# First mixer's convolution: 64x64 products in the four corners of the TensorE array, in place of 128x128 products

## The chip, the cores and the metric

The kernel runs on one core of one Trainium2 chip. The metric is the device time of one execution in microseconds (us). The profile is of one execution of the same program, taken by the hardware profiler. Engines are named as in the profile: PE is TensorE (products), PEld its loading of stationary operands, DVE is VectorE, ACT is ScalarE, POOL is GpSimd, and SP is the engine from whose queue nearly all DMAs are issued.

## The reference, cut to what matters

Two residual layers over 1024 positions of width 1024, float32. The first layer's mixer has two parallel parts, a convolution module and an mLSTM memory with four heads, behind one input projection and one output projection. What the change touches is the convolution module: 512 channels, each with a causal filter of 31 taps along the sequence, then a bias, a layer norm over the 512 channels and SiLU.

```python
z = h @ w_in
ca, cg, q, k, v, og, gates = jnp.split(z, cuts, -1)
u = ca * jax.nn.sigmoid(cg)
u = causal_depthwise_conv(u, conv_w, conv_b)      # 31 taps, one filter for each channel
u = jax.nn.silu(layernorm(u, ln_g, ln_b))
...
return jnp.concatenate([u, hm], -1) @ w_out
```

## The kernel before, in words

**The whole.** `trunk_kernel` runs `mixer0` (convolution and mLSTM), a feed-forward block, `mixer1` (gated linear attention), and a second feed-forward block. Almost all products are the projections: each operand is split into a high and a low part, and `mm3` (lines 174 to 176) adds three products for each pair, so that L174, L175 and L176 are the three products of one step of a projection. Weights come in with a DMA from SP (L164), ACT rounds them to the high part `wH` (L167) and DVE makes the low part `wL` (L168). The tags `wH` and `wL` have three buffers each.

**The order of the work.** `ORDER0` lists the steps of `mixer0`. Those that matter here are `c0` to `c3` (`conv_in`: the projection to 128 channels of `u`, and its store to DRAM), `v0` to `v3` (`conv`: the filter itself on these 128 channels), `g` (values and output gates of a head, `head_vo`, L548 and L549 read its banks), `x` (a head's recurrence, L623 to L645) and `l` (`layer_norm`). In `ORDER0` stand `v0 x0a v1 x0b g1` and later `v2 x1a v3 x1b l g2`. A scheduler in the language's layer turns program order and priorities (`high_priority`, offset `WOFF`) into one fixed list of instructions for each engine when the program is built. On the chip every engine works through its list in order and waits on semaphores.

**The filter as products.** Position t is 8n + s, with phase s from 0 to 7 and n from 0 to 127. `conv_in` stores `u` to DRAM as channel, phase, n (`ud`). `conv(i)` handles 128 channels in two halves `j` of 64. It loads a half as tile `ur`: 16 channels times 8 phases fill the 128 partitions, and four such groups lie side by side (L403; two buffers, `GB`). Taps reach back 30 positions, so at most four steps of n: for each group, five products (m from 0 to 4, L411) of a stationary 128x128 block with a 128-column window of `ur` shifted by m add up in PSUM. The stationary block maps (channel, phase in) to (phase out, channel). It is zero wherever the channels differ, so 15 of 16 of its elements are zero. The blocks of one group are a tile `cw` of 128x640 (L408), which takes a buffer of the tags `wH` and `wL` in turn. In all there are 4 (i) x 2 (j) x 4 (e) x 5 (m) = 160 products in float32 of 128x128 by 128 columns. Both operands are plain float32 here, and the trace shows each such product as two loads and two passes, so 320 rows. The four groups of a half fill one PSUM bank (`sm`, four buffers), which DVE reads with the bias (L413) into `y`.

**Behind it.** `layer_norm` sums over the channels by adding `y` tiles and by a product with `ones_p`, a matrix that says which partitions hold the same phase (built from `e4`, L359 to L365). The result goes to DRAM (`zd`, L449, 32 DMAs) and comes back channel-major (L455).

Of the kernel before, what the change touches and what calls it, by code (L numbers as in the profile page):

```python
# [8 lines left out]
F32 = mybir.dt.float32  # L9
# [7 lines left out]
P = 128  # L17
# [5 lines left out]
TAPS = 31  # L23
PH = 8
CG = 16
NT = T // PH
SH = 4
# [11 lines left out]
WOFF = 200  # L39
# [11 lines left out]
GB = 2  # L51
# [28 lines left out]
def trunk_kernel(ctx, tc, xT, cols, gate_b0, ev_vo0, ev_u, ev_cw, ev_out, od_v0, od_u, od_out, gate_w2, fin_row,  # L80
# [13 lines left out]
    def nm(s):  # L94
        uid[0] += 1
        return f"{s}_{uid[0]}"

    def bank(tag):
        return ps.tile([P, 512], F32, tag=tag, name=nm(tag))
# [7 lines left out]
    b = bank("sm")  # L107
# [186 lines left out]
    def mixer0(cut, then):  # L294
        with tc.tile_pool(name="m0", bufs=1, reuse_waits="tile") as mp:
# [62 lines left out]

            e4 = mp.tile([PH, PH, CG], F32, tag="e4", name="e4")  # L359
            DVE.tensor_copy(e4, ident[:PH, :PH].unsqueeze(2).to_broadcast([PH, PH, CG]))  # L360
            b = bank("sm")[:, :P]
            e4 = e4.rearrange("e a c -> e (a c)")
            PE.matmul(b, e4, e4, start=True, stop=True)
# [29 lines left out]
            def conv(i):  # L393


                for j in range(2):
                    b = bank("sm")
                    y = xy(2 * i + j if i < 2 else 2 * i + j - 4, int(i > 1))
                    Y.append(y)
                    with tc.high_priority(offset=WOFF):  # L400
                        raw = mp.tile([P, 4, NT + SH], F32, tag="ur", name=nm("ur"), bufs=GB)
                        DVE.memset(raw[:, :, :SH], 0.0)
                        SP.dma_start(raw[:, :, SH:], ud[i][j * 64:(j + 1) * 64].rearrange("(g c) s n -> (c s) g n", g=4))  # L403
                    for e in range(4):
                        g = 8 * i + 4 * j + e
                        with tc.high_priority(offset=WOFF):
                            w = wp.tile([P, 1088], F32, tag="wL" if e % 2 else "wH", name=nm("cw"))[:, :(SH + 1) * P]
                            SP.dma_start(w, ev_cw[g])  # L408
                        o = b[:, e * NT:(e + 1) * NT]
                        for m in range(SH + 1):  # L410
                            PE.matmul(o, w[:, m * P:(m + 1) * P], raw[:, e, m:m + NT], start=m == 0, stop=m == SH)  # L411
                    g = 8 * i + 4 * j
                    DVE.tensor_tensor(out=by_phase(y), in0=by_phase(b),  # L413
                                      in1=col[:, C_CB + g:C_CB + g + 4].unsqueeze(2).to_broadcast([P, 4, NT]), op=ALU.add)
# [11 lines left out]
            def layer_norm():  # L426
# [19 lines left out]
                for j, y in enumerate(Y):  # L446
                    DVE.tensor_tensor(out=by_phase(y), in0=by_phase(y), in1=r.unsqueeze(1).to_broadcast([P, 4, NT]), op=ALU.mult)
                    for e in range(4):
                        SP.dma_start(zd[4 * j + e].rearrange("c a n -> a c n"), y[:, e * NT:(e + 1) * NT])  # L449

# [1408 lines left out]
def _layout(i):  # L1859
# [17 lines left out]
    def phased(v):  # L1877

        return np.tile(v.reshape(-1, CG).T, (PH, 1))


    cw = i["ev_conv_w"][0].reshape(TAPS, 32, CG)
    band = np.zeros((32, CG, PH, SH + 1, PH, CG), np.float32)
    for c in range(CG):
        for m in range(SH + 1):
            for sp in range(PH):
                for ap in range(PH):
                    j = PH * (m - SH) + sp - ap + TAPS - 1
                    if 0 <= j < TAPS:
                        band[:, c, sp, m, ap, c] = cw[j, :, c]  # L1890
    band = band.reshape(32, P, (SH + 1) * P)
    qw = i["ev_qk_conv_w"][0].reshape(4, 8, P).transpose(2, 1, 0).reshape(P, 32)
# [4 lines left out]
    e = i["ev_w_in"][0]  # L1897
# [91 lines left out]
```

## Time and profile before

| | |
|---|---|
| median of 3 runs | 2112.51 us (2112.13 to 2113.88) |
| the profiled execution, device time | 2112.64 us |
| the profiled execution, span from first to last instruction | 2110.9 us |
| granted TensorE clock over the span | 0.998 |
| the filter's products (L411) on PE, in four pieces | 150.4 to 171.6 us and 221.3 to 242.4 us |
| passes of the filter on PE | 320 |
| DMAs of the filter's weights (`cw`) | 32 of 320 KB |
| DMAs of the filter's input (`ur`) | 8 of 256 KB |

A row of the groups reads: line, engine, operation, tile written and tiles read (buffer numbers left out), shapes, count, then busy time in us and the mean of one in ns, then the idle time of the engine just ahead. Products are pipelined, so the duration of one pass (some 275 ns) is longer than the distance from one pass to the next. That distance is what counts, and it is taken from the timeline, where rows of one line that follow each other are merged: start, length of the whole piece, and count. The length runs from the first start to the last end.

### The profile page before, as it was taken

Reading aid. Unit: us, or ns where it says so; the run is one execution under the profiler, and the core shown is the slowest. Engines: PE = TensorE matmul, PEld = TensorE weight load, DVE = VectorE, ACT = ScalarE, POOL = GpSimd, SP = SyncE. Lnnn points to the kernel's source line nnn. Section 1 sums busy time; section 2 is a strip of 40 time slices with the busy share of each in tenths; the row PEclk is TensorE's granted clock in tenths of the full one; section 3 lists DMA queues with packets and bytes.
Section 4 is the critical chain, followed back from the end, with each engine's and each line's share of the span. In section 5 each row is a group of like instructions: output and inputs, shape, how many; then the busy total and the mean of one; then the engine's idle time right before and its main releaser. Section 6 shows DMA issues by size and latency. Waiting matters only on the chain.

```text
span 2110.9 us, 27850 instructions
## 1 busy us (share of the span) xinstructions
PE 2094.3 (99%) x10367; PEld 1773.9 (84%) x10367; DVE 1508.4 (71%) x2296; ACT 866.7 (41%) x1411; POOL 2.9 (0%) x15
## 2 busy tenths in 40 slices
PE   9999999999999999999999999999999999999998
PEld 8889989888888888888889978888888888888887
DVE  7555788677776666867875577666877666677686
ACT  6212327443222232444546545644522232234553
POOL 0000000000000000000000000000000000000000
PEclk9999999999999999999999999999999999999999
DMA  4324454545443233834546643454544333374344
GB/s 157 96 98 136 148 129 121 200 167 178 169 156 109 90 105 131 293 97 133 165 133 218 201 146 119 170 179 149 190 155 166 114 105 110 101 273 145 96 129 146
DMA packets 154636, 312.57 MB, mean 148 GB/s; under 512 B 24128, under 2 KB 37312, under 8 KB 154496
## 3 DMA queue, kind: packets, MB, share of 16 engines
q1 hardware_dynamic: 154224, 310.48, 44.5%
q8 instruction: 83, 1.36, 0.3%
q14 instruction: 57, 0.47, 0.1%
q10 hardware_dynamic: 272, 0.26, 0.0%
HBM read 229.91 MB, written 80.77 MB: 147 GB/s over the span
## 4 chain that ended last, share of the span: by engine, by line
PE 96%; ACT 1%; DVE 1%; DMA 1%; issue 0%; SPq 0%; DVEq 0%; ACTq 0%
PE mm L174 20%; PE mm L175 20%; PE mm L176 20%; PE sm L176 10%; PE sm L174 10%; PE sm L175 10%; PE sm L411 2%; PE sm L1266 1%; PE sm L1268 1%; PE sm L1265 0%; DVE bs L1053 0%; PE sm L624 0%; PE sm L1293 0%; PE sm L1254 0%; PE sm L591 0%; PE sm L626 0%
## 5 line engine op out<-in xcount | busy, mean ns | idle before, releaser
L175 PE MATMUL mm<-hL,wH 128*128 128x512 f32 x1356 | 531.3, 392 | 0.3 <-DVE hL L339 0.3
L176 PE MATMUL mm<-hH,wH 128*128 128x512 f32 x1356 | 529.5, 391 | 0.0
L174 PE MATMUL mm<-hH,wL 128*128 128x512 f32 x1356 | 492.9, 392 | 3.4 <-ACT hH L338 1.5
L174 PEld LDWEIGHTS mm<-hH,wL 128*128 128x128 f32 x1356 | 254.5, 188 | 58.4 <-ACT hH L338 2.3
L175 PEld LDWEIGHTS mm<-hL,wH 128*128 128x128 f32 x1356 | 255.1, 188 | 53.2 <-DVE hL L339 0.6
L176 PEld LDWEIGHTS mm<-hH,wH 128*128 128x128 f32 x1356 | 254.9, 188 | 53.2 <-issue 0.2
L175 PE MATMUL sm<-hL,wH 128*128 128x512 f32 x616 | 240.1, 390 | 0.0
L176 PE MATMUL sm<-hH,wH 128*128 128x512 f32 x616 | 239.7, 389 | 0.0
L174 PE MATMUL sm<-hH,wL 128*128 128x512 f32 x616 | 209.0, 390 | 0.0
L147 ACT ACTIVATE wH<-S 128x1024 fp32r<-128x1024 f32 x97 | 102.8, 1060 | 232.9 <-PE sm L176 213.6
L147 ACT ACTIVATE wH<-q 128x512 fp32r<-128x512 f32 x143 | 90.3, 632 | 179.2 <-PE mm L176 98.8
L147 DVE TENSOR_TENSOR wL<-q,wH 128x512 fp32r<-128x512 f32 x143 | 98.6, 690 | 70.6 <-ACT wH L147 70.3
L147 ACT ACTIVATE wH<-raw 128x1024 fp32r<-128x1024 f32 (+1 forms) x90 | 89.9, 1000 | 122.2 <-PE sm L176 68.1
L147 DVE TENSOR_TENSOR wL<-S,wH 128x1024 fp32r<-128x1024 f32 x97 | 118.5, 1221 | 26.3 <-ACT wH L147 26.3
L175 PEld LDWEIGHTS sm<-hL,wH 128*128 128x128 f32 x616 | 115.6, 188 | 24.7 <-issue 0.7
L174 PEld LDWEIGHTS sm<-hH,wL 128*128 128x128 f32 x616 | 115.6, 188 | 24.5 <-PE mm L176 0.5
L176 PEld LDWEIGHTS sm<-hH,wH 128*128 128x128 f32 x616 | 115.6, 188 | 24.3 <-issue 0.2
L175 PE MATMUL mm<-wL,hH 128*128 128x256 f32 (+2 forms) x480 | 136.0, 284 | 0.0
L176 PE MATMUL mm<-wH,hH 128*128 128x256 f32 (+2 forms) x480 | 135.9, 285 | 0.0
L174 PE MATMUL mm<-wH,hL 128*128 128x256 f32 (+2 forms) x480 | 135.8, 286 | 0.1
L1493 DVE TENSOR_TENSOR c<-sm,c 128x512 f32<-128x512 f32 x110 | 75.6, 687 | 72.0 <-PE sm L176 72.0
L147 DVE TENSOR_TENSOR wL<-raw,wH 128x1024 fp32r<-128x1024 f32 (+1 forms) x90 | 103.5, 1150 | 13.2 <-ACT wH L147 13.2
(355 smaller groups left out, 3577.2 us busy)
## 6 DMA issues: line engine op xcount, KB each, us to landing
raw<-in_w SPq DMA_DIRECT2D x108, 512.0 KB
mdT<-c SPq DMA_DIRECT2D x88, 256.0 KB
m<-mdT SPq DMA_DIRECT2D x88, 256.0 KB
mdB<-c SPq DMA_DIRECT2D x66, 256.0 KB
raw<-in_od_u SPq DMA_DIRECT2D x32, 512.0 KB
q<-in_w SPq DMA_DIRECT2D x60, 256.0 KB
m<-mdB SPq DMA_DIRECT2D x55, 256.0 KB
raw<-in_ev_u SPq DMA_DIRECT2D x20, 512.0 KB
```

The lines of the kernel that those rows point to most:

```text
L147: ins = ACT.activation(dst[0], src, AF.Copy), lo.tensor_tensor(out=dst[1], in0=src, in1=dst[0], op=ALU.subtract)
L174: return (PE.matmul(o, lt[1], rt[0], start=start and not on, stop=False, skip_group_check=on), PE.matmul(o, lt[0], rt[1], start=False, sto ...
L175: PE.matmul(o, lt[0], rt[1], start=False, stop=False, skip_group_check=on),
L176: PE.matmul(o, lt[0], rt[0], start=False, stop=stop, skip_group_check=on))
L411: PE.matmul(o, w[:, m * P:(m + 1) * P], raw[:, e, m:m + NT], start=m == 0, stop=m == SH)
L1266: PE.matmul(ob[:, cc, :], A[:, cs], v[:, c, :], start=True, stop=st is None)
L1268: PE.matmul(ob[:, cc, :], q[:, cs], st, start=False, stop=True)
L1493: DVE.tensor_tensor(out=out, in0=a, in1=b, op=ALU.add)
```

## The change

Each product now has 64 rows and 64 columns of the array. Eight channels times eight phases fill 64 partitions; the block is still zero where channels differ (7 of 8 elements). The two halves `j` of `conv(i)` are no longer worked one after the other. They lie on partitions 0 to 63 and 64 to 127 of one tile `ur` with one buffer (128 x 8 groups x 132), loaded by two DMAs of 64 partitions. For each of four weight tiles (`e`) and each m, four products follow: two groups of eight channels (`hc`), which write partitions 0 to 63 or 64 to 127 of a bank, times two halves (`j`), which write one bank each. So the four products of a step use the four corners of the array. In all there are 4 x 4 x 5 x 2 x 2 = 320 products of 64x64 by 128 columns, in place of 160 of 128x128. There are 16 DMAs of weights of 128x640 in place of 32. The two banks of a `conv(i)` are finished together. Partitions of `y` are now (channel, phase) in place of (phase, channel), and `e4`, the bias columns and the store to `zd` follow that.

```diff
-            e4 = mp.tile([PH, PH, CG], F32, tag="e4", name="e4")
-            DVE.tensor_copy(e4, ident[:PH, :PH].unsqueeze(2).to_broadcast([PH, PH, CG]))
+            e4 = mp.tile([PH, CG, PH], F32, tag="e4", name="e4")
+            DVE.tensor_copy(e4, ident[:PH, :PH].unsqueeze(1).to_broadcast([PH, CG, PH]))
...
             def conv(i):
-                for j in range(2):
-                    b = bank("sm")
+                with tc.high_priority(offset=WOFF):
+                    raw = mp.tile([P, 8, NT + SH], F32, tag="ur", name=nm("ur"), bufs=1)
+                    DVE.memset(raw[:, :, :SH], 0.0)
+                    for j in range(2):
+                        SP.dma_start(raw[64 * j:64 * j + 64, :, SH:],
+                                     ud[i][64 * j:64 * j + 64].rearrange("(g c) s n -> (c s) g n", g=8))
+                bs = [bank("sm") for _ in range(2)]
+                for e in range(4):
+                    with tc.high_priority(offset=WOFF):
+                        w = wp.tile([P, 1088], F32, tag="wL" if e % 2 else "wH", name=nm("cw"))[:, :(SH + 1) * P]
+                        SP.dma_start(w, ev_cw[4 * i + e])
+                    for m in range(SH + 1):
+                        for hc in range(2):
+                            for j, b in enumerate(bs):
+                                rows = slice(64 * j, 64 * j + 64)
+                                o = (hc * (SH + 1) + m) * 64
+                                PE.matmul(b[64 * hc:64 * hc + 64, e * NT:(e + 1) * NT], w[rows, o:o + 64],
+                                          raw[rows, 2 * e + hc, m:m + NT], start=m == 0, stop=m == SH)
+                for j, b in enumerate(bs):
                     y = xy(2 * i + j if i < 2 else 2 * i + j - 4, int(i > 1))
                     Y.append(y)
-                    with tc.high_priority(offset=WOFF):
-                        raw = mp.tile([P, 4, NT + SH], F32, tag="ur", name=nm("ur"), bufs=GB)
-                        DVE.memset(raw[:, :, :SH], 0.0)
-                        SP.dma_start(raw[:, :, SH:], ud[i][j * 64:(j + 1) * 64].rearrange("(g c) s n -> (c s) g n", g=4))
-                    for e in range(4):
-                        g = 8 * i + 4 * j + e
-                        with tc.high_priority(offset=WOFF):
-                            w = wp.tile([P, 1088], F32, tag="wL" if e % 2 else "wH", name=nm("cw"))[:, :(SH + 1) * P]
-                            SP.dma_start(w, ev_cw[g])
-                        o = b[:, e * NT:(e + 1) * NT]
-                        for m in range(SH + 1):
-                            PE.matmul(o, w[:, m * P:(m + 1) * P], raw[:, e, m:m + NT], start=m == 0, stop=m == SH)
...
-                        SP.dma_start(zd[4 * j + e].rearrange("c a n -> a c n"), y[:, e * NT:(e + 1) * NT])
+                        SP.dma_start(zd[4 * j + e].rearrange("c a n -> (c a) n"), y[:, e * NT:(e + 1) * NT])
...
-    cw = i["ev_conv_w"][0].reshape(TAPS, 32, CG)
-    band = np.zeros((32, CG, PH, SH + 1, PH, CG), np.float32)
-    for c in range(CG):
+    cw = i["ev_conv_w"][0].reshape(TAPS, 4, 2, 4, 2, CG // 2).transpose(0, 1, 3, 2, 4, 5)
+    band = np.zeros((4, 4, 2, CG // 2, PH, 2, SH + 1, CG // 2, PH), np.float32)
+    for c in range(CG // 2):
...
-                        band[:, c, sp, m, ap, c] = cw[j, :, c]
-    band = band.reshape(32, P, (SH + 1) * P)
+                        band[:, :, :, c, sp, :, m, c, ap] = cw[j, ..., c]
+    band = band.reshape(16, P, 2 * (SH + 1) * 64)
```

The scheduler also gives PE another order around the filter. Behind the change, line numbers from 417 on are higher by four. The first place is PE's list from the end of `conv(0)` to the start of `conv(1)`; `ur_1443` is `conv(1)`'s input before. Before:

```order
L411 MATMUL sm_1364<-ur_1366,cw_1390 128x128 x5
L623 MATMUL sm_1398<-v_436,kw_1328 128x129
L624 MATMUL sm_1399<-v_436,rb_1307 128x129 x2
L623 MATMUL sm_1419<-v_436,kw_1328 128x129
L624 MATMUL sm_1420<-v_436,rb_1307 128x129
L623 MATMUL sm_1398<-v_436,kw_1328 128x129
L626 MATMUL sm_1399<-st_1402,qk_1067 128x129
L626 MATMUL sm_1420<-st_1407,qk_1067 128x129
L624 MATMUL sm_1420<-v_436,rb_1307 128x129
L411 MATMUL sm_1441<-ur_1443,cw_1446 128x128 x5
```

After, the last products of `conv(0)` and what follows them; `wH_1634` and `wL_1635` are the first weights of `head_vo(1)`:

```order
L411 MATMUL sm_1335<-ur_1330,cw_1402 64x128
L627 MATMUL sm_1428<-v_436,kw_1328 128x129
L628 MATMUL sm_1429<-v_436,rb_1307 128x129 x2
L174 MATMUL mm_1650<-wH_1634,hL_26_156 128x256
L174 MATMUL mm_1677<-wH_1634,hL_26_156 128x256
L174 MATMUL mm_1704<-wH_1634,hL_26_156 128x256
L174 MATMUL mm_1731<-wH_1634,hL_26_156 128x256
L627 MATMUL sm_1449<-v_436,kw_1328 128x129
L175 MATMUL mm_1650<-wL_1635,hH_25_155 128x256
L176 MATMUL mm_1650<-wH_1634,hH_25_155 128x256
```

So 48 of the 192 products of `head_vo(1)` now stand between the two pieces of the filter (42 of them behind the last row shown), beside the nine products of the recurrence that stood there before. The same holds for `head_vo(2)` between `conv(2)` and `conv(3)`.

The second place is DVE's list behind `conv(0)`; `sm_1334` and `sm_1335` are its two banks. Before, the reads of the banks (L413) and the clearing of the next inputs' margins (L402), with `conv(1)`'s banks `sm_1441` and `sm_1475`, and the low weights of `head_vo(1)`:

```order
L413 TENSOR_TENSOR xy_220_1442<-sm_1441,col 128x512
L402 MEMSET ur_1989 128x4x4
L168 TENSOR_TENSOR wL_1575<-raw_1572,wH_1574 128x1024
L431 TENSOR_TENSOR s_2229<-s_2229,xy_220_1442 128x512
L168 TENSOR_TENSOR wL_1581<-raw_1578,wH_1580 128x1024
L413 TENSOR_TENSOR xy_227_1476<-sm_1475,col 128x512
```

After, right behind `conv(0)`:

```order
L417 TENSOR_TENSOR xy_198_1424<-sm_1334,col 128x512
L397 MEMSET ur_1471 128x8x4
L168 TENSOR_TENSOR wL_1635<-raw_1632,wH_1634 128x1024
L417 TENSOR_TENSOR xy_199_1426<-sm_1335,col 128x512
L633 COPY st_1432<-sm_1428 128x129
```

The low part `wL` of the first weights of `head_vo(1)` has moved from the middle of `conv(1)` to the end of `conv(0)`, between the reads of `conv(0)`'s two banks. Its buffer is that of the last weights of `conv(0)` (`cw_1402`), so it cannot be written before `conv(0)` is through.

The third place is SP's list of DMAs, from the last weights of `conv(0)` on. Before, weights and input halves alternate:

```order
L408 DMA cw_1446<-in_ev_cw 128x640
L403 DMA ur_1443<-ud 128x4x128
L408 DMA cw_1453<-in_ev_cw 128x640
L408 DMA cw_1460<-in_ev_cw 128x640
L408 DMA cw_1467<-in_ev_cw 128x640
L408 DMA cw_1480<-in_ev_cw 128x640
L403 DMA ur_1477<-ud 128x4x128
```

After, all weights of `conv(1)` come first, and both halves of its input (`ur_1471`) together, when `conv(0)` has read the only buffer for the last time:

```order
L405 DMA cw_1499<-in_ev_cw 128x640
L405 DMA cw_1477<-in_ev_cw 128x640
L405 DMA cw_1521<-in_ev_cw 128x640
L391 DMA ud<-u_1195 128x1024
L405 DMA cw_1543<-in_ev_cw 128x640
L399 DMA ur_1471<-ud 64x8x128 x2
L164 DMA raw_1868<-in_ev_u 128x1024
```

Behind the tail of `mixer0` the lists of all engines are the same as before but for a few neighbouring products of one projection that change places.

More of the change, by code (lines that the diff above doesn't have):

```diff
@@ L357, in mixer0 @@
                                pattern=[[1, P]], channel_multiplier=-1)
-            e4 = mp.tile([PH, PH, CG], F32, tag="e4", name="e4")
-            DVE.tensor_copy(e4, ident[:PH, :PH].unsqueeze(2).to_broadcast([PH, PH, CG]))
+            e4 = mp.tile([PH, CG, PH], F32, tag="e4", name="e4")
+            DVE.tensor_copy(e4, ident[:PH, :PH].unsqueeze(1).to_broadcast([PH, CG, PH]))
             b = bank("sm")[:, :P]
-            e4 = e4.rearrange("e a c -> e (a c)")
+            e4 = e4.rearrange("e c a -> e (c a)")
             PE.matmul(b, e4, e4, start=True, stop=True)
@@ L1877, in phased @@
     def phased(v):
-        return np.tile(v.reshape(-1, CG).T, (PH, 1))
-    cw = i["ev_conv_w"][0].reshape(TAPS, 32, CG)
-    band = np.zeros((32, CG, PH, SH + 1, PH, CG), np.float32)
-    for c in range(CG):
+        return np.repeat(v.reshape(-1, CG).T, PH, axis=0)
+    cw = i["ev_conv_w"][0].reshape(TAPS, 4, 2, 4, 2, CG // 2).transpose(0, 1, 3, 2, 4, 5)
+    band = np.zeros((4, 4, 2, CG // 2, PH, 2, SH + 1, CG // 2, PH), np.float32)
+    for c in range(CG // 2):
         for m in range(SH + 1):
```

## The prediction

> **What bounds the kernel.** First the page's busy times and the shares of the chain of work that ended last:
>
> ```profile
> PE 2094.3 (99%) x10367; PEld 1773.9 (84%) x10367; DVE 1508.4 (71%) x2296; ACT 866.7 (41%) x1411; POOL 2.9 (0%) x15
> PE 96%; ACT 1%; DVE 1%; DMA 1%; issue 0%; SPq 0%; DVEq 0%; ACTq 0%
> ```
>
> PE is the chain: of 2110.9 us of span it lacks only 16.6 us. Next the stretch in which the filter runs, 150 to 260 us, in the table by stage (busy PE, PEld, DVE, ACT, POOL, then granted clock, DMA share, GB/s), and the shares of the chain from 140 to 260 us:
>
> ```profile
> 150.00:260.00 110.00, 109.56 (x854) 105.12 (x853) 65.47 (x143) 27.58 (x77) 0.00 (x0) 1.00 0.49 156
> by line: PE sm L411 29.8%; PE mm L176 18.9%; PE mm L175 18.9%; PE mm L174 18.8%; PE sm L624 3.3%; PE sm L591 3.0%; PE sm L626 2.7%; PE sm L623 2.6%; PE sm L596 1.3%; DVE st L632 0.6%; PE sm L424 0.2%; issue 0.1%
> ```
>
> PE stands still for 0.44 us there, at full clock, and L411, the filter, holds 29.8% of 120 us, 35.8 us. DVE is busy for 60% and so has room. So a nanosecond of PE time won or lost in the filter is one of the whole, until something else is late.
>
> **The filter's passes.** The timeline of PE gives the distance from pass to pass, and the groups of instructions (shapes kept apart) the duration of one:
>
> ```profile
> 150.43 9.10 PE L411 MATMUL sm<-ur,cw 128*128 128x128 f32 x80
> 150.00 0.60 PE L596 MATMUL sm<-ident,qk 128*128 128x128 f32 x4
> 78.78 0.78 PE L518 MATMUL sm<-ident,row 4*128 4x4 f32 x10
> 78.78 0.69 PEld L518 LDWEIGHTS sm<-ident,row 4*128 4x128 f32 x10 [0.35 <-issue]
> ```
> ```profile
> L411 PE MATMUL sm<-ur,cw 128*128 128x128 f32 x320 | 36.7, 275 | 0.0
> L1266 PE MATMUL sm<-v,A 128*128 128x256 f32 x64 | 18.5, 379 | 0.0
> L411 PEld LDWEIGHTS sm<-ur,cw 128*128 128x128 f32 x320 | 36.2, 192 | 0.0
> L596 PEld LDWEIGHTS sm<-ident,qk 128*128 128x128 f32 x28 | 3.3, 141 | 0.0
> L489 PEld LDWEIGHTS sm<-ident,gz 128*36 128x36 f32 x8 | 0.7, 98 | 0.2
> L1063 PEld LDWEIGHTS sm<-ident,least 128*1 128x1 f32 x1 | 0.1, 84 | 0.0
> L518 PEld LDWEIGHTS sm<-ident,row 4*128 4x128 f32 x24 | 1.9, 136 | 2.0 <-issue 1.4 <-DVE wL L168 0.4 <-DVE row L512 0.2
> ```
>
> Of the first row, the last pass alone takes 0.275 us, so 79 distances fill 9.10 - 0.275 us: 111.7 ns each (112 below), and 320 of them make 35.7 us. Two things ask for these 112 ns. A pass of 256 columns takes 104 ns more than one of 128 (379 against 275), so 128 columns stream for some 104 ns. The load of 128 float32 columns takes 192 ns where that of one column takes 84, so 108 ns are the columns, 0.85 ns each. Load and stream lie beside each other, or the distance would be twice as long. Both are full.
>
> The change makes 640 passes and 640 loads of 64 columns. A stream is as long as before (128 columns). A load has 84 + 64 x 0.85 = 138 ns, which is what L518's load has (136; a transpose loads a column in about half the time: 98 ns for 36 columns, 141 for 128). L518's products have four columns, so its row shows such loads with next to nothing beside them: (0.69 - 0.136) / 9 = 62 ns from load to load. All columns to be loaded together are as many as before (640 x 64 = 320 x 128). The change halves the streams, if four run at a time, but not the loads. Four cases follow for the filter's 35.7 us:
>
> (a) Loads go one after the other, as in every row of the trace: 640 x 62 ns = 39.7 us, 4.0 us more.
> (b) Loads of different corners overlap, but products start in order. A float32 product is two passes in one corner (320 rows for 160 products). The second waits for the first's 104 ns, and the next product's first pass can go beside it, no earlier. So one product per 111.7 ns: 320 x 111.7 ns = 35.7 us, nothing gained.
> (c) Every corner goes its own way: 80 rounds of two passes at 111.7 ns, 17.9 us, a gain of 17.9 us.
> (d) Nothing overlaps: 640 x 111.7 ns = 71.5 us, 35.7 us more.
>
> I take (a). It needs no behaviour that the trace does not show, L518 is the nearest row, and where (a) and (b) both hold the slower one counts. Its ends are (b)'s 35.7 us and 39.7 us.
>
> The Trainium skill (TensorE: Matmul & The Clock Gate, Part 3, on packing small matmuls) has products in different corners start about 4 ns apart and run side by side. That taken alone gives (c). The same section has products start and finish strictly in program order, which with two passes in one corner gives (b). Neither is shown by a run here, and the trace has no two products that share the array.
>
> **Changing the shape.** PE goes into the 64x64 products and out of them ten times (twice around each `conv`, once more because a first product of `conv(1)` stands alone). The trace has no such change; the nearest is from L518's loads of four rows to a full projection:
>
> ```profile
> 79.49 0.50 PE L175 MATMUL mm<-hL,wH 128*128 128x512 f32 x1
> ```
>
> L518's last pass starts 0.198 us (its duration) before its piece ends at 79.56, so at 79.36; the projection starts 0.13 us on, about its load's 108 ns. So I take nothing. The other end is that a pass must be through before the next load begins, 275 - 112 = 163 ns each, 1.6 us. The Trainium skill (TensorEngine Tiling (Array Packing), Tiling Modes, Key Properties) says that changing the tiling mode drains TensorE; by it the sum is those 1.6 us higher. No row here shows it.
>
> **The new order around the filter.** Behind `conv(0)` PE now runs a product L623 and two of L624 (six passes of 112 ns), four L174 of 256 columns, another L623, and then an L175 that needs `wL_1635`. DVE makes that between the reads of the two banks.
>
> ```profile
> 173.05 0.28 PE L174 MATMUL mm<-wH,hL 128*128 128x256 f32 x1
> 174.96 0.28 PE L175 MATMUL mm<-wL,hH 128*128 128x256 f32 x1
> 159.59 0.67 DVE L413 TENSOR_TENSOR xy<-sm,col 128x512 f32<-128x512 f32 x1 [3.79 <-issue]
> 160.18 0.28 DVE L629 COPY st<-sm 128x129 f32<-128x129 f32 x1
> L168 DVE TENSOR_TENSOR wL<-raw,wH x67: 1199/1225/1294, 24.1 to 1455.9; 128x1024 fp32r<-128x1024 f32 x63, 128x1056 fp32r<-128x1056 f32 x2, 128x1088 fp32r<-128x1088 f32 x2
> PE sm L626 <- DVE st L632: 0.4, 2, 0.2
> ```
>
> Sixteen projection passes take 1.91 us, 0.12 each. So PE reaches the L175 8 x 0.112 + 4 x 0.12 = 1.4 us after the filter's last start. DVE begins the bank read when that pass has ended (9.10 us after 150.43, at 159.53, the read at 159.59), some 0.33 us after its start; 0.6 us later (159.59 to 160.18) it goes on, and L168 takes 1.23 us: 2.15 us. PE waits 0.75 us. `conv(2)` has the same order, so 1.5 us in all. In return the two waits of 0.2 us for the recurrence (last row) are covered by projections: 1.1 us net. The ends: nothing, if PE comes late anyway, and 1.6 us.
>
> **What costs nothing, and why.** There are 16 weight DMAs fewer (16 x 320 KB), but PE waited for no DMA here. `ur` has one buffer, so `conv(1)`'s input is asked for only when `conv(0)` has read its own:
>
> ```profile
> 155.09 0.73 SPq L403 DMA_DIRECT2D ur<-ud  x1
> 162.08 2.17 PE L411 MATMUL sm<-ur,cw 128*128 128x128 f32 x18
> ```
>
> The old transfer took at most these 7.0 us. Now 48 projections (5.8 us), nine products of two passes (2.0 us) and the 0.75 us wait lie between, 8.5 us, of which about 1 us passes before the DMA goes (bank read, then clearing the margins). So 7.5 us cover 7.0. If the two halves take longer than that, PE waits for the rest, and the weights queued behind on SP come later by as much, but `head_vo(1)` needs them only after `conv(1)`. Both banks are read at the end, so the recurrence's banks come free about 1.9 us later (L168 and a read); that is under the 42 projections (5 us). The stores to `zd` are as many and as large as before, on SP alone; `e4` is of the same size. From the tail of the mixer on the lists are alike.
>
> **The sum.** +4.0 for the filter, 0 for changes of shape, +1.1 for the order: +5.1 us. The profiled execution took 2112.64 us, 1.74 us of it outside its span, which the change doesn't touch; it is 0.13 us above the median. So 2112.64 + 5.1 = 2117.7 us, slower by 0.24%. What a measurement of this kernel can tell from no change is about 0.2%, 4.2 us. The forecast's own range: 2112.6 (no term costs anything) to 2112.64 + 4.0 + 1.6 + 1.6 = 2119.8.
>
> **Rivals.**
> - *Streams set the pace, loads overlap,* case (b): 0 + 1.1, 2113.7 us, no change. For it: in the old filter load and stream are equally long, so it takes little for the streams to be the later ones. Against it: no row of the trace has two loads at once. Chance 0.25.
> - *The corners really go in parallel,* case (c): -17.9 + 1.1 = -16.8, 2095.8 us. It decides for faster by over 0.2% once passes come less than (35.7 - 4.2 - 1.1) / 640 = 47 ns apart. For it: the streams of a round share neither rows and columns nor banks. Against it: loads 62 ns apart (L518), and two passes of each product in one corner. Chance 0.22.
> - *The corners do not overlap at all,* case (d): the change doesn't do what it says, and each small pass costs what a large one did: +35.7 + 1.1, 2149.4 us. For it: no row shows two products at once, and PE's starts lie 104 ns or more apart wherever 128 columns stream. Against it: every load of the trace already lies beside a product, so the array does two things at a time. Chance 0.18.
>
> **How the numbers follow.** The forecast keeps 0.35. Of it 0.27 lies above 4.2 us and 0.08 within. Faster: 0.22 of (c) and 0.01 of (b), 0.23. Same: 0.24 of (b) and 0.08, 0.32. Slower: 0.27 and 0.18 of (d), 0.45. The range leaves out (d) alone: from just under (c), 2095, to just over the forecast's upper end, 2121.
>
> **What would show it.** In the changed profile, the length of a filter piece on PE over its 160 passes: 62 ns a pass for (a), 56 for (b), 28 for (c), 112 for (d). Of the new waits: about 0.75 us of PE idle at L175, released by DVE L168, behind `conv(0)` and `conv(2)`. At the first L411 of `conv(1)` and `conv(3)` no idle released by a DMA. Around the pieces, a distance over 0.2 us from the last small pass to the next full one would show the price of the change of shape. The forecast is wrong if passes come under 56 or over 64 ns apart, or if PE waits for `ur`.

## The result, and the profile after

| | before | after |
|---|---|---|
| median | 2112.32 us (2111.36 to 2113.88, 4 runs) | 2099.43 us (2098.65 to 2103.08, 4 runs) |
| profiled execution, device time | 2112.64 us | 2098.65 us |
| its span | 2110.9 us | 2096.9 us |

The ratio is 0.9945, 95% interval 0.9933 to 0.9956: faster by 0.55%, some 12 us. The forecast was 2117.7 us, slower by 0.24%: the direction was wrong. The time lies within the range that was given, but near its other end, close to the rival (c), 2095.8 us.

The page of the changed kernel, busy times and the chain of work that ended last:

```profile
PE 2076.3 (99%) x10687; PEld 1753.5 (84%) x10687; DVE 1507.4 (72%) x2292; ACT 865.5 (41%) x1411; POOL 2.9 (0%) x15
PE 95%; DVE 2%; ACT 2%; DMA 1%; issue 0%; SPq 0%; DVEq 0%; ACTq 0%
```

PE still is the chain and has 320 passes more, but is busy for 18.0 us less (2094.3 before). Its span shrank by 14.0 us only, so it also stands still for longer. The filter's products and loads (all rows of one line: shortest, median and longest in ns):

```profile
L411 PEld LDWEIGHTS sm<-ur,cw x640: 129/133/133, 148.9 to 231.0; 64*64 64x64 f32 x160
L411 PE MATMUL sm<-ur,cw x640: 267/269/321, 148.9 to 231.1; 64*64 64x128 f32 x160
```

The load takes 133 ns, where 138 were estimated, and the pass 269 ns, where it took 275 before. What changed is the distance. The timeline of PE around `conv(0)` (start, length of the piece, and at the end of a row its passes and the idle time ahead with its releaser):

```profile
148.36 0.60 PE L600 MATMUL sm<-ident,qk 128*128 128x128 f32 x4
148.89 4.60 PE L411 MATMUL sm<-ur,cw 64*64 64x128 f32 x160
153.42 0.49 PE L627 MATMUL sm<-v,kw 128*128 128x129 f32 x2
155.43 0.38 PE L175 MATMUL mm<-wL,hH 128*128 128x256 f32 x1 [0.38 <-DVE wL L168]
162.00 0.43 PE L411 MATMUL sm<-ur,cw 64*64 64x128 f32 x2
163.00 4.61 PE L411 MATMUL sm<-ur,cw 64*64 64x128 f32 x158
```

(4.60 - 0.269) / 159 = 27.2 ns a pass. Four times 27.2 is 109: each corner has its own rhythm of one pass in 109 ns, and four of them run at once. That is case (c). 640 x 27.2 ns = 17.4 us stand against 35.7, a gain of 18.3 us. The single starts show the rounds. These are the first rows of the piece in the timeline, cut off at 148.92, at 149.04 and at 149.08 us:

```profile
148.89 0.34 PE L411 MATMUL sm<-ur,cw 64*64 64x128 f32 x4
148.89 0.34 PE L411 MATMUL sm<-ur,cw 64*64 64x128 f32 x4
148.89 0.45 PE L411 MATMUL sm<-ur,cw 64*64 64x128 f32 x8
```

Four passes start within 20 ns of the first one, 6 to 7 ns apart. The second four follow 160 ns behind the first four, and from there on each four follow 109 ns behind the four before. A product is two passes in one corner, so in the list three second passes stand ahead of the fourth start, and they do not hold it up. What took part of the gain back is in the list of PE's waits (us in total, times, longest); of before, `L174 <- DVE wL` had 1.2 us and `L175 <- DVE wL` no row:

```profile
PE mm L174 <- DVE wL L168: 3.3, 3, 2.4
PE mm L174 <- DVE least L1059: 2.5, 1, 2.5
PE mm L175 <- DVE wL L168: 2.3, 4, 0.9
PE sm L109 <- DVE t L106: 1.6, 1, 1.6
...
PE mm L174 <- ACT hH L338: 0.6, 1, 0.6
```

and in the table by stage for the stretch of the filter (busy PE, PEld, DVE, ACT, POOL, clock, DMA share, GB/s):

```profile
150.00:260.00 110.00, 107.17 (x1237) 99.69 (x1230) 71.85 (x155) 34.09 (x94) 0.00 (x0) 1.00 0.39 112
```

PE stands still for 2.83 us there, 0.44 before. DVE has 65% of this stretch where it had 60%: with PE ahead of its old time, 155 of DVE's operations fall into it, 143 before.

### The profile page after: what moved, and what is told of

Read it like the earlier page. It is cut to its first block, busy times and chain, and to the rows that moved or that the text cites. A ratio compares the mean times of both kernels' runs of the same rounds, so it can differ in the third digit from the quotient of the medians.

```text
span 2096.9 us, 28455 instructions
## 1 busy us (share of the span) xinstructions
PE 2076.3 (99%) x10687; PEld 1753.5 (84%) x10687; DVE 1507.4 (72%) x2292; ACT 865.5 (41%) x1411; POOL 2.9 (0%) x15
## 4 chain that ended last, share of the span: by engine, by line
PE 95%; DVE 2%; ACT 2%; DMA 1%; issue 0%; SPq 0%; DVEq 0%; ACTq 0%
PE mm L175 20%; PE mm L174 20%; PE mm L176 20%; PE sm L176 10%; PE sm L174 10%; PE sm L175 10%; PE sm L1270 1%; PE sm L1269 1%; PE sm L1272 1%; DVE wL L168 0%; DVE bs L1057 0%; DMA rb<-rowd 0%; PE sm L1297 0%; PE sm L1258 0%; PE sm L630 0%
## 5 line engine op out<-in xcount | busy, mean ns | idle before, releaser
L175 PE MATMUL mm<-hL,wH 128*128 128x512 f32 x1356 | 530.9, 392 | 0.5 <-DVE hL L339 0.4
L174 PE MATMUL mm<-hH,wL 128*128 128x512 f32 x1356 | 492.4, 392 | 4.6 <-DVE wL L168 3.3
L174 PEld LDWEIGHTS mm<-hH,wL 128*128 128x128 f32 x1356 | 254.2, 188 | 60.1 <-DVE wL L168 3.4
L175 PEld LDWEIGHTS mm<-hL,wH 128*128 128x128 f32 x1356 | 254.6, 188 | 53.5 <-DVE hL L339 1.1
L175 PE MATMUL sm<-hL,wH 128*128 128x512 f32 x616 | 240.1, 390 | 0.0
L174 PE MATMUL sm<-hH,wL 128*128 128x512 f32 x616 | 209.0, 390 | 0.0
L175 PE MATMUL mm<-wL,hH 128*128 128x256 f32 (+2 forms) x480 | 136.0, 285 | 2.3 <-DVE wL L168 2.3
L175 PEld LDWEIGHTS sm<-hL,wH 128*128 128x128 f32 x616 | 115.6, 188 | 24.7 <-issue 0.7
L174 PEld LDWEIGHTS sm<-hH,wL 128*128 128x128 f32 x616 | 115.6, 188 | 24.4 <-PE mm L176 0.5
L174 PE MATMUL mm<-wH,hL 128*128 128x256 f32 (+2 forms) x480 | 135.4, 287 | 0.5 <-ACT wH L167 0.3
```

The source lines that it names most:

```text
L174: return (PE.matmul(o, lt[1], rt[0], start=start and not on, stop=False, skip_group_check=on), PE.matmul(o, lt[0], rt[1], start=False, sto ...
L175: PE.matmul(o, lt[0], rt[1], start=False, stop=False, skip_group_check=on),
```

## The experiments

The theory after the result: (1) each corner of the array works through its own passes, and the gain is the overlap alone; (2) part of it is lost to changes of shape and to waits for low weights. The rivals: the gain comes from fewer DMAs or from the new order; passes overlap only where their order in the list allows it; the loss is something else.

**The old shape in the new order (`e1_full`).**

```diff
                     for m in range(SH + 1):
-                        for hc in range(2):
-                            for j, b in enumerate(bs):
-                                rows = slice(64 * j, 64 * j + 64)
...
+                        for j, b in enumerate(bs):
+                            PE.matmul(b[:, e * NT:(e + 1) * NT], w[:, m * P:(m + 1) * P],
+                                      raw[:, 2 * e + j, m:m + NT], start=m == 0, stop=m == SH)
```

> The changed kernel with its order of work, its DMAs and its buffers, but each step of the filter as two products of 128x128 (one for each half, 320 passes in all) in place of four of 64x64. Both halves then get wrong taps: the filter's values are not the reference's, all sizes are. Theory (the gain comes from corners that run side by side): passes 112 ns apart, filter 35.7 us, and the time goes back to the kernel before or a little over it, 2111 to 2116 us. Rival (the gain comes from half the weight DMAs or from the projections that now lie between the pieces): it stays at 2099 to 2104 us although the passes are 112 ns apart.

Measured: 2114.46 us, 1.0016 of before (1.0006 to 1.0026). So DMAs and order bring nothing; alone they cost 2.8 us by the medians (1.3 to 5.5 by the interval; the profiled span is 0.7 us longer than that of before). Two rows of its timeline, a whole piece of the filter and the longest wait of its projections:

```profile
219.60 9.10 PE L408 MATMUL sm<-ur,cw 128*128 128x128 f32 x80
349.81 0.50 PE L174 MATMUL mm<-hH,wL 128*128 128x512 f32 x1 [2.45 <-DVE wL L168]
```

The piece is as long as before, 9.10 us. The wait of 2.45 us stands in the mixer's tail, at the first weights of the output projection. The changed kernel has it too (2.4 above), before has not (its longest for `wL` was 0.6). Since it comes with the order even when the filter is as slow as before, it is not the short filter that makes it. DVE's list has three long operations (L660) ahead of that L168:

```profile
333.44 1.88 DVE L660 TENSOR_TENSOR xy<-xy,ssq 128x512 f32<-128x512 f32 x3
335.24 0.35 DVE L552 TENSOR_SCALAR v<-mm,rt 128x128 f32<-128x128 f32 x1
335.50 1.22 DVE L168 TENSOR_TENSOR wL<-raw,wH 128x1024 fp32r<-128x1024 f32 x1
336.77 0.51 PE L174 MATMUL mm<-hH,wL 128*128 128x512 f32 x1 [2.35 <-DVE wL L168]
```

These rows are of the changed kernel. Why the scheduler puts L168 there was not taken further.

**Who takes turns with whom (`e2_single`, `e3_rows`, `e4_cols`).** All products are the same; only the three loops over `m`, `hc` (columns) and `j` (rows and banks) are nested in other ways: `hc`, `j`, `m` in `e2_single` (shown), `hc`, `m`, `j` in `e3_rows`, and `j`, `m`, `hc` in `e4_cols`.

```diff
-                    for m in range(SH + 1):
-                        for hc in range(2):
-                            for j, b in enumerate(bs):
+                    for hc in range(2):
+                        for j, b in enumerate(bs):
+                            for m in range(SH + 1):
```

> The changed kernel with the same 320 products, but within a weight tile the five steps of one corner follow each other before the next corner has its turn. Theory A (a pass that cannot start yet holds up all that are behind it in the list): ten passes in a row in one corner, 112 ns a pass, a piece of 160 passes takes 17.9 us in place of 4.6, the kernel 2099 + 53 less the waits that are covered again, 2145 to 2153 us. Theory B (each corner has its own queue, long enough for ten passes): as the changed kernel, 27 ns a pass, 2099 us. In between (a short queue): between 27 and 112 ns.

> The changed kernel with the same products, only two corners taking turns: the two halves, that is the two row groups, at the same columns and in two banks; the other columns follow after five steps. Corners side by side as far as the order lets them: 55 ns a pass, a piece of 160 passes 8.9 us, the kernel 2099 + 17.9 less up to 4.4 us of waits that are covered again, 2112 to 2117 us. If row groups do not overlap, 112 ns and 2145 to 2153 us. If the queue reaches ten products ahead, 27 ns and 2099 us.

> The changed kernel with the same products, only two corners taking turns: the two column groups, at the same rows and into one bank; the other half follows after five steps. Corners side by side as far as the order lets them: 55 ns a pass, a piece of 160 passes 8.9 us, 2112 to 2117 us. If products in the same rows, or into the same bank, hold each other up, 112 ns and 2145 to 2153 us, while the turns between the two row groups still give 55 ns.

Measured: 2126.82, 2104.89 and 2103.97 us (one run each; before in the same job 2111.7). The pieces of `conv(0)` in this order:

```profile
149.53 11.98 PE L411 MATMUL sm<-ur,cw 64*64 64x128 f32 x160
```
```profile
150.19 6.35 PE L411 MATMUL sm<-ur,cw 64*64 64x128 f32 x160
```
```profile
149.47 6.36 PE L411 MATMUL sm<-ur,cw 64*64 64x128 f32 x160
```

With the last pass's 0.27 us taken off that is 73.6, 38.2 and 38.3 ns a pass. The first stands between the two theories, where a short queue was put; the others lie under the 55 ns that two corners side by side would give. With ten passes in a row in one corner it should have been 109 ns if nothing overlapped, and 99 if a pass could start only behind all that stand ahead of it in the list (nine distances of 109 ns in a corner, then one short step to the next: 988 ns for ten). 73.6 says that the next corner begins about three passes before the last one is through. The starts in the trace of `e2_single` show it. These are its first rows, the timeline cut off at 150.235 and at 150.24 us:

```profile
149.53 0.98 PE L411 MATMUL sm<-ur,cw 64*64 64x128 f32 x7
149.53 1.03 PE L411 MATMUL sm<-ur,cw 64*64 64x128 f32 x8
```

Seven passes start one after the other (the second 160 ns behind the first, the others some 109 ns apart), the eighth only 6 ns behind the seventh, and then two starts fall into each 109 ns for three rounds. The records do not name the corner. But read with the list, the eighth start is the next corner's first, while three passes of the first corner still wait, and these run in the three rounds. Two corners taking turns come to 38 for the same reason: the next two begin early. Row groups in two banks and column groups in one bank do not differ.

That gives a model: passes are issued in the list's order; each corner takes in a few passes beyond the one that runs; issue stops only where a corner is full. With two such passes it gives 78.8 and 40.8 ns for the two kinds of order, with three 68.5 and 36.0. It was put to the test with two orders it had not seen.

**Two and three products in a row (`e12_two`, `e13_three`).** The diff is the first's; the other has the groups (0, 1, 2) and (3, 4).

```diff
-                    for m in range(SH + 1):
+                    for ms in ((0, 1), (2, 3), (4,)):
                         for hc in range(2):
                             for j, b in enumerate(bs):
...
+                                for m in ms:
...
```

> The changed kernel with the same products, but two products (four passes) of one corner follow each other before the next corner has its turn, the fifth step alone. A model made from the two orders already seen: passes are issued in the order of the list, each corner takes in two or three passes beyond the one that runs, and issue stops only where a corner is full. With two it gives 78.8 ns a pass for ten in a row and 40.8 for two row groups taking turns, with three 68.5 and 36.0 (measured 73.6 and 38.2). For this order it gives 30 ns with two and 27 with three: a piece of 160 passes 4.6 to 5.1 us, 2099 to 2102 us. Strict order of all passes would give about 97 ns a pass and over 2130 us.

> The same with three products of one corner in a row, then two. The model gives 46.6 ns a pass with two waiting passes for each corner and 35.6 with three, in the mean 41: a piece of 160 passes 5.9 to 7.7 us, 2103 to 2109 us. If the queue were one for all corners and longer than twelve passes: 27 ns.

Measured: 2101.68 and 2105.69 us (one run each). The pieces:

```profile
149.81 4.76 PE L412 MATMUL sm<-ur,cw 64*64 64x128 f32 x160
```
```profile
149.02 6.74 PE L412 MATMUL sm<-ur,cw 64*64 64x128 f32 x160
```

28.2 and 40.7 ns a pass, both between the model's values for two and three (27 to 30, 36 to 47). The starts decide between the two. In `e12_two` the first four starts lie 13 ns apart, though each time three passes of the corner before stand between them in the list. In `e13_three` the next corner begins at the third start of a corner that has six in a row. With `e2_single` that makes three waiting passes in all three orders. What the model left out is the first pass of a corner that stood idle, which holds up the second by 51 ns more (160 ns in place of 109). With three waiting passes and these 51 ns the model gives 73.6, 38.5, 27.6 and 40.7 ns for ten in a row, two corners taking turns, four in a row, and six and four; measured were 73.6, 38.2, 28.2 and 40.7. This fit was made with the measurements known, so it is no forecast. The overlap needs turns between the corners, but not pass by pass: four passes in a row (one that runs, three that wait) cost almost nothing, six cost much (40.7 against 27.2 ns).

**Loads or streams (`e8_half`).**

```diff
                     for m in range(SH + 1):
+                        n = NT // 2 if m else NT
...
-                                PE.matmul(b[64 * hc:64 * hc + 64, e * NT:(e + 1) * NT], w[rows, o:o + 64],
-                                          raw[rows, 2 * e + hc, m:m + NT], start=m == 0, stop=m == SH)
+                                PE.matmul(b[64 * hc:64 * hc + 64, e * NT:e * NT + n], w[rows, o:o + 64],
+                                          raw[rows, 2 * e + hc, m:m + n], start=m == 0, stop=m == SH)
```

> The changed kernel with half the columns streamed in four of five steps (64 in place of 128); the taps left out make the filter's values other than the reference's. It tells what sets the 109 ns of a round. If the streams: 0.6 of the columns, a piece of 160 passes takes 4.6 x 0.6, 2.8 us, some 16 to 17 ns a pass. If a corner's load, which does not shrink with the columns: 4.5 us as in the changed kernel. The kernel gains up to 7 us by the first, of which the waits for low weights may take most.

Measured: 2096.97 us (one run).

```profile
149.57 2.97 PE L412 MATMUL sm<-ur,cw 64*64 64x128 f32 x160
```

(2.97 - 0.22) / 159 = 17.3 ns, 0.64 of 27.2 for 0.6 of the columns. The starts of 64-column passes of one corner lie 58 ns apart where those of 128 columns lie 109 apart, with loads as long as before (135 ns). So the streams set the pace at 128 columns, and the loads are hidden behind them. The four pieces are 6.5 us shorter than in the changed kernel, and the kernel by 2.5 us; with one run, which lies 1.7 us below the fastest of the changed kernel's four, that is not clear of their spread of 4.4 us. Of the rest, PE's waits show a part: 1.9 us for high weights (L167) and 2.3 us for operands of L628 stand in the list, and the granted clock is 0.5 for 3.4 us from 218.9 us on.

**The price of a change of shape (`e9_mix`).**

```diff
                     for m in range(SH + 1):
+                        if m % 2 == 0:
+                            for j, b in enumerate(bs):
+                                PE.matmul(b[:, e * NT:(e + 1) * NT], w[:, m * P:(m + 1) * P],
+                                          raw[:, 2 * e + j, m:m + NT], start=m == 0, stop=m == SH,
+                                          skip_group_check=True)
+                            continue
                         for hc in range(2):
...
-                                          raw[rows, 2 * e + hc, m:m + NT], start=m == 0, stop=m == SH)
+                                          raw[rows, 2 * e + hc, m:m + NT], start=False, stop=False,
+                                          skip_group_check=True)
```

> The price of changing the shape: of the five steps of each weight tile the first, third and fifth are two products of 128x128, the second and fourth four products of 64x64, so that PE changes its shape four times in each of 16 tiles, 64 times in all instead of ten. The taps are mixed up, so the filter's values are not the reference's. A piece of four tiles has 48 passes of 112 ns and 64 of 27 ns, 7.1 us. If a change costs nothing, a piece takes 7.1 us. If it costs what the first pass behind the filter shows in the changed kernel (0.2 us late), the eight changes back to the large shape in a piece, or the sixteen in all, add 1.6 to 3.2 us: 8.7 to 10.3 us.

Measured: 2123.33 us (one run). Full products (L409) and small ones (L417) take turns:

```profile
152.34 1.16 PE L409 MATMUL sm<-ur,cw 128*128 128x128 f32 x8
153.43 0.45 PE L417 MATMUL sm<-ur,cw 64*64 64x128 f32 x8
153.81 0.71 PE L409 MATMUL sm<-ur,cw 128*128 128x128 f32 x4
```

From 152.34 to 153.81 are 1.47 us. Eight full passes take 0.89 (111.7 ns each) and eight small ones 0.22 (27.2). The rest, 0.36 us, is the price of one change to the small shape and one back. The whole piece of `conv(0)` lasts 10.1 us, within the 8.7 to 10.3 that a price was to give, and not 7.1. The changed kernel has five such pairs, 1.8 us. The rows of its own timeline agree: the last pass of L600 starts 0.27 us before its piece ends at 148.96, and the first small pass is recorded 0.2 us after that start, at 148.89; the last small pass starts 0.27 us before 153.49, and the next full one 0.2 us after it, at 153.42. The Trainium skill (TensorEngine Tiling (Array Packing), Tiling Modes, Key Properties) says that a change of tiling mode drains TensorE; these rows agree, and the pair costs about three passes.

**Buffers for the filter's weights (`e5_owncw`, `e10_cw3h`, `e10_cw3l`).** Behind the filter, L175 waits for low weights whose buffer was the filter's last weight tile. The first of three versions takes the tiles out of these tags:

```diff
-                        w = wp.tile([P, 1088], F32, tag="wL" if e % 2 else "wH", name=nm("cw"))[:, :(SH + 1) * P]
+                        w = mp.tile([P, (SH + 1) * P], F32, tag="cw", name=nm("cw"), bufs=3)
```

> The changed kernel with one edit: the filter's weight tiles have three buffers of their own in place of those of the projections' weights. The low weights of head_vo(1) are then made before the reads of the filter's banks. Theory (4 us of the gain went into PE's waits for low weights, because these take the buffer of the filter's last weights): the waits of L175 behind the filter's pieces, 2.3 us in all, go, and the kernel takes 2096.5 to 2098 us. Rival (PE then waits as long at the next place, for DVE has as much to do): 2099 us, with the waits moved.

Measured: 2113.23 us, 1.001 of before (1.0001 to 1.002). Both theories missed on the time: the waits of L175 for low weights did go, but a longer one came. PE's longest wait, one of the pieces, and the table by stage around that piece:

```profile
PE sm L411 <- DMA cw<-in_ev_cw: 12.5, 4, 4.9
```
```profile
158.92 2.41 PE L411 MATMUL sm<-ur,cw 64*64 64x128 f32 x40 [4.85 <-DMA cw<-in_ev_cw]
```
```profile
158.90:161.40 2.50, 2.48 (x41) 2.15 (x41) 0.01 (x1) 0.00 (x0) 0.00 (x0) 0.50 0.22 86
```

The fourth tile's DMA can go only when the first has been read, and takes about 5 us where the products of all three tiles take 3.5. The six buffers shared with the projections had hidden that. The wait costs more than its own time: behind it the granted clock is 0.5, and the 40 passes lie 55 ns apart, twice the 27.2. Behind each of the four waits the trace has such a stretch of 3.4 us, which can make up to 6.8 us more (estimated from half of four times 3.4).

In the other two the fourth tile goes back to one of the shared tags, `wH` in `e10_cw3h` and `wL` in `e10_cw3l`:

```diff
-                        w = mp.tile([P, (SH + 1) * P], F32, tag="cw", name=nm("cw"), bufs=3)
+                        w = mp.tile([P, (SH + 1) * P], F32, tag="cw", name=nm("cw"), bufs=3) if e < 3 else \
+                            wp.tile([P, 1088], F32, tag="wH", name=nm("cw"))[:, :(SH + 1) * P]
```

> As e5_owncw (three weight buffers of the filter's own), but the fourth weight tile of each group takes a buffer of the tag wH, so that no weight tile waits for the first one to be read. Theory (what e5_owncw lost was its 12.5 us of waiting for weight DMAs, and the low weights of head_vo(1), now made ahead of the banks' reads, no longer hold up L175): no wait for cw, the waits of L175 for low weights (2.3 us in the changed kernel) gone, one change of shape less in conv(1): 2096.5 to 2098.5 us, 0.993 of before. Rival (the cover is short everywhere, and DVE is late elsewhere by as much): 2099 to 2101 us.

> The same with the fourth weight tile in a buffer of the tag wL. The second low weights of head_vo(1) are then made between the reads of the two banks. Theory: a little behind the kernel with wH, 2097 to 2100 us, with waits for low weights of 0.5 to 1.5 us behind the filter's pieces. Rival: as the changed kernel, 2099 to 2101 us.

Measured: 2100.70 us for `wH`, 0.9951 of before (0.9938 to 0.9965), and 2095.39 us for `wL`, 0.9923 (0.9909 to 0.9936). So of the two the one that was thought a little behind is ahead. With `wH` the wait moves to the filter's input:

```profile
PE sm L412 <- DMA ur<-ud: 1.7, 3, 0.8
```

That is the single buffer of `ur`, whose cover was put at 7.5 us for a transfer of up to 7.0. With `wL` there are eight projections more (56 in place of 48) between `conv(0)` and `conv(1)` in PE's list, no small piece of two passes, and in the stretch of the filter PE has no gap at all:

```profile
150.00:260.00 110.00, 110.00 (x1288) 103.37 (x1287) 75.96 (x164) 31.94 (x92) 0.00 (x0) 1.00 0.39 116
```

The waits of L175 for `wL` are gone (2.3 us in the changed kernel); those of L174, most of them in the tail, stay at 3.2 us. This version is ahead of the kernel before. Ahead of the changed kernel it is by 4 us in the medians, but each is measured against runs of the kernel before of its own, the two intervals just touch (0.9933 and 0.9936), and the profiled spans differ by 1.2 us. So that it beats the changed kernel is not shown.

**Sixteen corners (`e6_32`).** The tiles are cut once more: four channels, 32 rows and columns, four row groups in four banks.

```diff
...
-                        for hc in range(2):
-                            for j, b in enumerate(bs):
-                                rows = slice(64 * j, 64 * j + 64)
...
+                        for hc in range(4):
+                            for q, b in enumerate(bs):
+                                rows = slice(32 * q, 32 * q + 32)
...
```

> The filter in 32x32 products: four channels times eight phases, 640 products, 1280 passes, sixteen corners taking turns, four banks for each group of 128 channels, 8 DMAs of weights. The values are the reference's. Theory (each corner goes its own way; starts lie 7 ns apart within a round): sixteen starts fill the round of 109 ns, 7 to 8 ns a pass, so the filter takes 9 to 10 us in place of 17.5; the kernel 2099 - 8 = 2091 us, less what waits take back, 2091 to 2097 us. Rival (one start costs more than 7 ns as soon as there is no pause between the rounds, or loads of 32 rows do not overlap): 14 ns or more a pass, 17.9 us or more, and the kernel no faster than the changed one, 2099 us or over.

Measured: 2113.12 us, 1.0008 of before (0.9999 to 1.0017). The filter of `conv(0)` on PE:

```profile
148.79 1.89 PE L411 MATMUL sm<-ur,cw 32*32 32x128 f32 x102
151.54 2.61 PE L411 MATMUL sm<-ur,cw 32*32 32x128 f32 x141 [0.86 <-DVE kw L612]
156.29 1.32 PE L411 MATMUL sm<-ur,cw 32*32 32x128 f32 x77 [2.14 <-issue]
```

(2.61 - 0.27) / 140 = 16.7 ns a pass (13.8 in the last row), not 7, and there are 1280: the rival's case. Added to that are pauses for which the profile names no releaser ("issue"), 7.8 us over the kernel. Together the filter of `conv(0)` lasts 8.8 us (148.79 to 157.61) in place of 4.6.

The trace points at a cause of the pauses that this list of waits can't name. One DMA queue carries instructions. Its packets, MB and share, before and in `e6_32`:

```profile
q8 instruction: 83, 1.36, 0.3%
```
```profile
q8 instruction: 90, 1.47, 0.3%
```

Each packet has 16 KB, and there is one for every 125 to 126 of PE's passes in both kernels (10367 and 11327 passes), so they are most likely PE's own instructions. In `e6_32` such a packet has landed 1.2 to 1.5 us before the end of each of the four pauses (at 154.89 us for the pause that ends at 156.29), and 1.5 and 1.6 us before the end of the pauses of this kind at the filter in `e10_cw3h` and `e8_half`. In the filter of `e6_32` the packets come 3.4 us apart at the closest, which is 27 ns for each of 126 passes. So PE probably waited for its instructions; smaller products would then gain nothing over a long stretch. No run varied it, and what limits the passes between the pauses to 13 to 17 ns (the four banks, the loads) stays open too.

## Why the prediction was wrong

**The step that failed** is the choice of case (a): "It needs no behaviour that the trace does not show, L518 is the nearest row, and where (a) and (b) both hold the slower one counts." L518's loads follow each other in the same four rows of the array, over all 128 columns, so their 62 ns say nothing about loads in four different corners. The filter's loads lie beside each other: 133 ns long, four of them begun within 20 ns, one per 27.2 ns in the mean. The 4.0 us were to be a loss, and the term was a gain of 18.3. `e8_half` shows that loads do not set the pace.

**Case (b)** failed by its premise too, that products start in order. The changed kernel's own starts tell it (four corners within 20 ns), and `e2_single`: 73.6 ns a pass where strict order allows 99 at best. A second pass that must wait in its corner does not hold up the passes of other corners as long as no more than three wait there. So of PE it is not true, as was said ahead of the prediction, that an engine works through its list in order: between corners the starts change places. Of the Trainium skill, the rule that speaks for (c) is also in TensorEngine Tiling (Array Packing), Tiling Modes, Key Properties: different tiles load and multiply in parallel; the trace agrees with its 27.2 ns. The rule of strict order (TensorE: Matmul & The Clock Gate, Part 3), which gave (b), does not hold for the starts of these products.

**The chances.** (c) had 0.22 for want of a row with two products at once. But the lack of a row spoke no more for (a), whose row was one of a single place in the array; where no row bears on the question, the cases should have stood about even, and the likeliest should not have been the one with the handiest number. The argument for (c) that the streams of a round share no bank was not so: the two column groups of a half write the same bank, and `e4_cols` shows that this costs nothing (38.3 against 38.2 ns).

**Changes of shape**: taken as nothing, end 1.6 us; measured 0.36 us a pair, five pairs, 1.8 us. The row from L518 to L175, which stood for it, showed none of this price, so it was no measure of it.

**The order**: +1.1 us. `e1_full` gives +2.8 by the medians, between 1.3 and 5.5; the direction was right. The wait at L175 behind `conv(0)` and `conv(2)` came, at 0.38 and 0.58 us for the 0.75 each that were put down, but also behind the other two, 2.3 us in all. What was missed stands far from the filter: 2.4 us in the mixer's tail. "From the tail of the mixer on the lists are alike" passed over the place of one L168.

**What was put at nothing**: in the changed kernel PE waits for no DMA at the filter, so the single buffer of `ur` and the weights were rightly free. That the cover was thin is shown by `e10_cw3h`, which lost 1.7 us there.

**The sum as it is now**: -18.3 for the passes, +1.8 for the shape, and +3.5 for PE's waits (the rows of the list add up to 9.0 us before and 12.5 after) make -13.0 us; the spans differ by 14.0. The remaining 1.0 us has no row of its own. The rival (c), -16.8 us, had the right mechanism, and its price for shape and waits was 1.1 us where it is 5.3.

## What to carry to other kernels

Where a stationary block is mostly zeros, products in the corners of the array pay: four times the passes per time, of which this filter needs twice as many, so that its time on PE halves. That holds as long as the list lets the corners take turns at least every four passes and as long as PE does not change shape often (0.36 us for in and out). A duration or distance measured with one resource busy (loads into the same rows) is no bound for work on four corners. And when the engine that sets the time gets faster, look at what was prepared behind its back: here PE's waits took 3.5 us of the 18.3, mostly for operands that DVE prepares. The waits at L175 are 2.3 us with the short filter and 0.7 in `e1_full` with the long one, and they went when the filter's tiles had buffers of their own (`e10_cw3l`); the wait in the tail came with the new order.

## What the runs showed of the hardware

- Four 64x64 corners run at one float32 pass of 128 columns per 109 ns each, 27.2 ns together; two row groups or two column groups give the same (38.2 and 38.3 ns in the same order of turns), also into one bank.
- PE's starts are not in the list's order across corners: a corner takes in three passes beyond the one that runs (from the starts of `e2_single`, `e12_two` and `e13_three`; 73.6, 40.7, 38.2 and 28.2 ns a pass for ten in a row, six and four, two corners taking turns, and four in a row).
- Going into the small shape and back costs 0.36 us in all.
- Sixteen 32x32 corners came to one pass per 13 to 17 ns here, with four pauses of 0.5 to 2.9 us, each of which ended 1.2 to 1.5 us after a 16 KB packet of the instruction queue had landed.
- Behind waits of PE of 2.35 to 4.85 us the granted clock was 0.5 for 3.4 us (`e5_owncw`), and small passes lay 55 ns apart in place of 27.2.
